# Rooms of attention's first operands in SBUF reordered, and mLSTM steps begun 0.3 heads later

## The chip, the cores and the metric

One core of a Trainium2 chip runs the whole program, one decoder block over 2048 tokens. The metric is the time of one execution in microseconds (us). A core has five engines that work side by side: TensorE (PE, matmuls and transposes into PSUM), VectorE (DVE), ScalarE (ACT), GpSimd (POOL) and SyncE (SP), which here only issues DMA transfers. Each engine works through its own list of instructions strictly in order, and waits at the head of the list until what that instruction needs has happened.

## The reference, cut to what matters

The block computes a normalised hybrid mixer, a memory cross-attention and a mixture of experts:

```
z = rms_norm(x) @ w_in                      # input projection, split into
aq, ak, av, mu, mv, mo, mi, mf = split(z)   # attention and mLSTM parts
y_att = dilated_attention(rope(aq), rope(ak), av)     # 8 heads of 64
hc = mlstm_chunkwise(q(conv(mu)), k(conv(mu)), mv, mi, mf)  # 4 heads of 128
y_m = sigmoid(mo) * (norm(hc) + skip * conv(mu))
x += concat(y_att, y_m) @ w_out
x += cross_attention(rms_norm(x), rms_norm(mem))
x += hierarchical_moe(rms_norm(x));  out = rms_norm(x)
```

An attention head mixes three causal windows: 128 keys at stride 1 (set A in the kernel: 16 blocks of 128 queries against at most 256 keys), and the strides 4 and 16 together (set B: 16 tiles in four residue classes). Each block is scores, mask, exponent, a transpose of the probabilities, and their product with v. The mLSTM group runs 16 steps (4 groups of chunks times 4 heads) that carry a state from group to group.

## The kernel before

Every large product is done in two halves of a number, high and low, so that three matmuls stand for one.

**Stages.** `in_proj` (line 84) computes z in two halves of the sequence and writes all its parts to DRAM scratch tensors. `heads` (line 832) then runs three things at once: `attention` (line 370), head after head; `mlstm` (line 689); and `out_m` (line 791), the mLSTM rows' share of the output projection, in two halves. `cross` and `experts` follow.

**Order.** A planner builds each engine's list: it simulates the engines and takes among the instructions whose inputs it believes ready the one of the lowest priority number. Attention is traced first, and `marks[h]` keeps the priority at which head h begins. `go(t, gen)` sets the priority to that of time t in heads (t = 2.5 is the middle of head 2) and runs one step of `mlstm` or `out_m` there. mLSTM steps stand at t = 5.5 i / 16, i = 0 to 15, steps of `out_m` from t = 2 to 7.3 and its second half up to 7.9. All loads and stores of these stages are issued by SP, in one list.

**Rooms.** A pool of tiles (`pool`, line 46) takes a stretch of each SBUF partition. Pools are stacked in the order in which they are opened, tags inside a pool in the order of their first use. The pools of `heads` lie on the bytes that the pools of `in_proj` left. With `reuse_waits="tile"` a tile waits only for the users of the earlier tiles on its own bytes. Worked out from the shapes, in KiB from the start of a partition (1 KiB of kept tiles lies first), `in_proj` left:

- 1 to 10: constants `p1c`, the identity matrix `a_ident` among them, which the gate rows' transposes (line 685) still read
- 10 to 22.6: weight stage `wr` (3 buffers); to 34.6: `xr` (3), one of which is `room1` of the small gate rows of `gates` (line 619)
- to 42.6: `sq` (2); to 43.6: `dg`; to 59.6: `qh`, `ql` (2 each), which the convolution uses last; to 61.7: `on`; to 65.7: `u`; to 69.7: `v`
- to 81.7: output tiles `o` (3), written by the output gates (`gate`, line 316) at the very end and stored to `z_mo` (line 325)
- to 131: weights `W`; to 205: the x splits `xh`, `xl`, read until the last gate matmul

Before the change `heads` lays on them: score and row tiles `p2s` (1 to 15), `kl0`, `kl1`, identity and masks (15 to 34.5), `PTA`, three pairs of transposed probabilities of set A (to 46.5), `qs`, `kk` of the even heads (to 62.5), `vA`, `vB` (to 78.5), `PTB` (to 98.5), `qs`, `kk` of the odd heads (to 114.5), and, last, the tiles of `out_m` and `mlstm`, on the x splits.

**Names.** `load_qk` (line 394) loads a head's `qs`, `kk` and `kl`, ten transfers of 256 KB. `kl` holds a zero half that POOL writes once (lines 391, 392). Line 438/439 are the score matmuls, 446 mask and maximum (DVE), 447 the exponent (ACT), 493 and 552 the transposes, 452/453 the copies into `PTA`/`PTB` (ACT the high half, DVE the low one), 511 and 564 the products with `vA`, `vB`. In an mLSTM step line 739 and 746 load, 755 is q times k, 761 a transpose, 770 to 774 the products.

Of the kernel before, what the change touches and what calls it, by code (L numbers as in the profile page):

```python
# [8 lines left out]
F32 = mybir.dt.float32  # L9
F32R = mybir.dt.float32r  # L10
# [5 lines left out]
P = 128  # L16
D = 1024
S = 2048
# [27 lines left out]
def pool(tc, ctx, name, bufs, space=None, side=None):  # L46
    kw = {} if space is None else {"space": space}
    return ctx.enter_context(tc.tile_pool(name=name, bufs=bufs, side=side, reuse_waits="tile", **kw))
# [321 lines left out]
def attention(tc, ctx, I, Z, K, marks):  # L370

    nc = tc.nc
    sp = pool(tc, ctx, "p2s", 2)
    cp = pool(tc, ctx, "p2c", 1)
    qp = [pool(tc, ctx, "p2q", 1)]
    vp = [pool(tc, ctx, "p2v" + x, 1) for x in "ab"]
    dp = pool(tc, ctx, "p2d", 1)
    qp.append(pool(tc, ctx, "p2r", 1))
    op = pool(tc, ctx, "p2o", 1)
# [2 lines left out]
    ps_o = pool(tc, ctx, "p2po", NO, PSUM)  # L382

    def const(name, shape):
        t = cp.tile(shape, F32, name="b_" + name)
        nc.sync.dma_start(t, I[name])
        return t


    kls = [cp.tile([P, S], F32R, name=f"kl{x}") for x in range(2)]  # L390
    nc.gpsimd.memset(kls[0].bitcast(F32)[64:128], 0.0)
    nc.gpsimd.memset(kls[1].bitcast(F32)[0:64], 0.0)

    def load_qk(h):

        kl = kls[h % 2]
        qs, kk = (qp[h % 2].tile([P, S], F32R, name=f"{n}{h}", tag=n) for n in ("qs", "kk"))
        rows = slice(h * 64, h * 64 + 64)
        own, other = (slice(x * 64, x * 64 + 64) for x in (h % 2, 1 - h % 2))
        for c in range(2):  # L400
            cs = slice(c * 1024, c * 1024 + 1024)
            nc.sync.dma_start(qs.bitcast(F32)[own, cs], Z["qkh"][0, rows, cs])
            nc.sync.dma_start(qs.bitcast(F32)[other, cs], Z["qkl"][0, rows, cs])
            for to in (own, other):
                nc.sync.dma_start(kk.bitcast(F32)[to, cs], Z["qkh"][1, rows, cs])
            nc.sync.dma_start(kl.bitcast(F32)[own, cs], Z["qkl"][1, rows, cs])
        return qs, kk, kl
# [10 lines left out]

    first = load_qk(0)
    ident, mA, mB = const("ident", [P, P]), const("maskA", [P, 256]), const("maskB", [P, 512])  # L420
    K["ident"] = ident

# [49 lines left out]
    for pair in range(4):  # L472
# [3 lines left out]
        for e in range(2):  # L476
            h = 2 * pair + e
            marks.append(tc.cur_priority)
            qs, kk, kl = load_qk(h) if h else first
# [61 lines left out]
            for r in range(4):  # L541
# [15 lines left out]
                for kt in range(4):  # L557
                    for x in range(2):
                        if kt == 0:
                            t = pt[x][:, 1]  # L560
# [271 lines left out]
def heads(tc, I, Z, K):  # L832

    marks = []
    with ExitStack() as ctx:
        attention(tc, ctx, I, Z, K, marks)
        pb = pool(tc, ctx, "p3pb", NB, PSUM)

        def go(t, gen):

            j = int(t)
            tc.cur_priority = marks[j] + int((marks[j + 1] - marks[j]) * (t - j))
            next(gen, None)

        with ExitStack() as c2:
            o = out_m(tc, ctx, I, Z, pb, 0, 1)
            next(o)
            m = mlstm(tc, c2, I, Z, K, pb)
            next(m)
            at = [(MEND * i / 16, 0, i) for i in range(16)] + [(OSTART + (OMID - OSTART) * i / 16, 1, i) for i in range(16)]  # L850
            done = 0
            for t, which, i in sorted(at):

                while which and done < min(16, i // 4 * 4 + 5):
                    go(t, m)
                    done += 1
                if which or i == done:
                    go(t, (m, o)[which])
                    done += not which
        o = out_m(tc, ctx, I, Z, pb, 1, 2)  # L860
        for i in range(17):
            go(OMID + (OEND - OMID) * i / 16, o)
        tc.cur_priority = max(marks[9], tc.cur_priority)
        return marks[8]
# [3 lines left out]
WARM = 9  # L868
NS, NT, NO, NB = 2, 2, 2, 2
NPA, NPB = 3, 2  # L870
MEND, OSTART, OMID, OEND = 5.5, 2, 7.3, 7.9


def mm3(nc, out, wh, wl, xh, xl, first, last):
# [973 lines left out]
def block_kernel(tc, I, out):  # L1848
    with ExitStack() as ctx:
        Z = scratch(tc, ctx)  # L1850
        K = keep(tc, ctx)
        in_proj(tc, I, Z, K)
        soon = heads(tc, I, Z, K)
        router = Router(tc, ctx, I, Z)
        cross(tc, I, Z, router, soon)
        experts(tc, I, Z, router, out)
# [14 lines left out]
```

## Time and profile before

| | us |
|---|---|
| median of 3 runs | 2208.98 (2201.88 to 2212.25) |
| the profiled execution | 2215.31 |
| its span | 2213.5 |

The page's busy line gives each engine's busy time, its share of the span and its instructions. A table by stage gives, for each stretch, its length, then busy time and count of PE, of the weight loads (PEld), DVE, ACT and POOL, then the mean granted clock of PE (1.00 is full speed), the mean busy share of the 16 DMA engines, and GB/s moved. A list of waits says which instruction stood for what. A timeline gives start, duration, engine, line, operands and count, and in brackets the idle time before it and what ended it.

### The profile page before, as it was taken

What the parts mean: (1) busy time and instruction counts of PE and PEld (TensorE: products, weight loads), DVE (VectorE), ACT (ScalarE), POOL (GpSimd) and SP (SyncE); (2) the same over time, 40 slices, a digit from 0 to 9 for tenths busy, and PEclk for the clock granted to TensorE, in tenths of its full rate; (3) what the DMA queues carried; (4) which work ended last, traced back from release to release, by engine and by line L of the source; (5) the groups of instructions that cost most, each with busy time, mean ns of one, the idle gap of its engine ahead of it and who ended that gap; (6) DMA issues with size and microseconds to landing.
All of it is one profiled execution on the core that took longest, in us unless ns stands there. A gap on an engine that the chain in (4) does not pass through costs nothing. (4 is left out here: it accounts for less than half of the span.)

```text
span 2213.5 us, 36146 instructions
## 1 busy us (share of the span) xinstructions
PE 2041.5 (92%) x13247; PEld 1875.2 (85%) x13247; DVE 1373.3 (62%) x3315; ACT 1043.4 (47%) x2216; POOL 635.0 (29%) x415
## 2 busy tenths in 40 slices
PE   8999999999888888889969999858999999999996
PEld 6898988988677888879968999857999998889985
DVE  8125741255278889865688788865666565445576
ACT  5223432233266766665534545425555554444462
POOL 3541235421344454543240020142111111121003
PEclk9999999999899999999979999968999999999998
DMA  7544645342697897786552222257878786666596
GB/s 205 178 154 142 215 144 155 113 131 111 174 236 195 242 234 216 208 228 182 180 175 72 100 96 87 87 156 239 247 222 251 202 240 193 168 188 179 152 337 236
DMA packets 276244, 402.45 MB, mean 182 GB/s; under 512 B 28176, under 2 KB 204624, under 8 KB 276016
## 3 DMA queue, kind: packets, MB, share of 16 engines
q1 hardware_dynamic: 262528, 355.11, 52.3%
q0 software_dynamic: 13536, 45.00, 8.3%
q8 instruction: 106, 1.74, 0.3%
q14 instruction: 74, 0.61, 0.1%
HBM read 286.33 MB, written 114.00 MB: 181 GB/s over the span
## 5 line engine op out<-in xcount | busy, mean ns | idle before, releaser
L39 POOL TENSOR_TENSOR wl<-wr,wh 128x1024 fp32r<-128x1024 f32 (+1 forms) x46 | 118.9, 2606 | 256.0 <-ACT wh L38 244.0
L1654 POOL DMA_INDIRECT z_acc<-y,ix x34 | 55.9, 1645 | 407.2 <-DVE y L1646 175.5
L876 PE MATMUL pa<-xl,ww_0h 128*128 128x256 f32 (+5 forms) x512 | 153.0, 307 | 2.2 <-DVE xl L42 2.2
L875 PE MATMUL pa<-xh,ww_1h 128*128 128x256 f32 (+5 forms) x512 | 152.0, 297 | 0.0
L877 PE MATMUL pa<-xh,ww_1l 128*128 128x256 f32 (+5 forms) x512 | 151.7, 296 | 0.0
L876 PE MATMUL pa<-xl,ww_1h 128*128 128x256 f32 (+5 forms) x512 | 151.6, 296 | 0.0
L877 PE MATMUL pa<-xh,ww_0l 128*128 128x256 f32 (+5 forms) x512 | 147.6, 299 | 0.0
L335 PE MATMUL pn<-wl,xh 128*128 128x256 f32 (+1 forms) x512 | 144.9, 283 | 0.0
L334 PE MATMUL pn<-wh,xh 128*128 128x256 f32 (+1 forms) x512 | 144.9, 283 | 0.0
L336 PE MATMUL pn<-wh,xl 128*128 128x256 f32 (+1 forms) x512 | 144.9, 283 | 0.0
L42 DVE SCALAR_TENSOR_TENSOR xl<-pt,f_gf,xh 128x256 fp32r<-128x256 f32 (+5 forms) x128 | 64.3, 515 | 116.5 <-ACT xh L41 116.1
L875 PE MATMUL pa<-xh,ww_0h 128*128 128x256 f32 (+5 forms) x512 | 135.4, 301 | 0.6 <-ACT xh L41 0.6
L41 ACT ACTIVATE xh<-pt,f_gf 128x256 fp32r<-128x256 f32 (+5 forms) x128 | 61.9, 499 | 135.6 <-PE pt L1576 135.2
L38 ACT CAST wh<-wr 128x1024 fp32r<-128x1024 f32 (+3 forms) x49 | 48.4, 1030 | 130.5 <-PE pn L336 58.0
L39 DVE TENSOR_TENSOR ww_1l<-ww_1r,ww_1h 128x512 fp32r<-128x512 f32 x124 | 77.6, 676 | 46.3 <-ACT ww_1h L38 46.2
L876 PEld LDWEIGHTS pa<-xl,ww_0h 128*128 128x128 f32 x512 | 97.8, 192 | 4.8 <-DVE xl L42 2.4
L877 PEld LDWEIGHTS pa<-xh,ww_0l 128*128 128x128 f32 x512 | 97.6, 192 | 0.9
L335 PEld LDWEIGHTS pn<-wl,xh 128*128 128x128 f32 x512 | 97.1, 190 | 0.9
L334 PEld LDWEIGHTS pn<-wh,xh 128*128 128x128 f32 x512 | 97.1, 190 | 0.9
L336 PEld LDWEIGHTS pn<-wh,xl 128*128 128x128 f32 x512 | 96.9, 189 | 0.5
L875 PEld LDWEIGHTS pa<-xh,ww_1h 128*128 128x128 f32 x512 | 97.4, 190 | 0.0
L877 PEld LDWEIGHTS pa<-xh,ww_1l 128*128 128x128 f32 x512 | 97.2, 190 | 0.0
(708 smaller groups left out, 7140.3 us busy)
## 6 DMA issues: line engine op xcount, KB each, us to landing
ww_1r<-w SPq DMA_DIRECT2D x31, 1024.0 KB
ww_0r<-w SPq DMA_DIRECT2D x30, 1024.0 KB
wr<-w_in SPq DMA_DIRECT2D x43, 512.0 KB
w_0r<-w SPq DMA_DIRECT2D x16, 1024.0 KB
w_1r<-w SPq DMA_DIRECT2D x16, 1024.0 KB
z_v<-v SPq DMA_DIRECT2D x32, 256.0 KB
z_mqk<-mq SPq DMA_DIRECT2D x16, 512.0 KB
kk<-z_qkh SPq DMA_DIRECT2D x32, 256.0 KB
```

The costliest lines, as they stand in the source:

```text
L38: a = nc.scalar.copy(hi, src)
L39: b = eng.tensor_sub(lo, src, hi.bitcast(F32))
L41: a = nc.scalar.activation(hi, src, AF.Copy, scale=scale)
L42: b = eng.scalar_tensor_tensor(lo, src, scale, hi.bitcast(F32), op0=OP.mult, op1=OP.subtract)
L334: nc.tensor.matmul(ps[:, :n], xhw, wh[:, k, :], start=(k == 0), stop=False)
L335: nc.tensor.matmul(ps[:, :n], xhw, wl[:, k, :], start=False, stop=False)
L336: nc.tensor.matmul(ps[:, :n], xlw, wh[:, k, :], start=False, stop=(k == KT - 1))
L875: nc.tensor.matmul(out, wh, xh, start=first, stop=False, skip_group_check=True)
L876: nc.tensor.matmul(out, wh, xl, start=False, stop=False, skip_group_check=True)
L877: nc.tensor.matmul(out, wl, xh, start=False, stop=last, skip_group_check=True)
L1654: d = nc.gpsimd.indirect_dma_start(out=Z["acc"], out_offset=bass.IndirectOffsetOnAxis(ap=self.ix[:r, n:n + 1], axis=0), in_=y[:r], in_offs ...
```

## The change

It opens three pools first, a new one (`ip`) for the `kl` tiles, the identity and the masks, then that of the even heads' `qs` and `kk`, then those of `vA` and `vB`; the score tiles and the pool of `PTA` come after them. All sizes stay, so everything from `PTB` on lies where it lay. The new places, in KiB: `kl0`, `kl1` 1 to 17, identity and masks to 20.5, `qs`, `kk` to 36.5, `vA` to 44.5, `vB` to 52.5, score tiles to 66.5, `PTA` to 78.5. And mLSTM steps stand at t = 0.3 + 5.2 i / 16. No instruction is added or removed.

```diff
 def attention(tc, ctx, I, Z, K, marks):
 
     nc = tc.nc
+
+    ip = pool(tc, ctx, "p2i", 1)
+    qp = [pool(tc, ctx, "p2q", 1)]
+    vp = [pool(tc, ctx, "p2v" + x, 1) for x in "ab"]
     sp = pool(tc, ctx, "p2s", 2)
     cp = pool(tc, ctx, "p2c", 1)
-    qp = [pool(tc, ctx, "p2q", 1)]
-    vp = [pool(tc, ctx, "p2v" + x, 1) for x in "ab"]
     dp = pool(tc, ctx, "p2d", 1)
...
     def const(name, shape):
-        t = cp.tile(shape, F32, name="b_" + name)
+        t = ip.tile(shape, F32, name="b_" + name)
...
-    kls = [cp.tile([P, S], F32R, name=f"kl{x}") for x in range(2)]
+    kls = [ip.tile([P, S], F32R, name=f"kl{x}") for x in range(2)]
...
-            at = [(MEND * i / 16, 0, i) for i in range(16)] + [(OSTART + (OMID - OSTART) * i / 16, 1, i) for i in range(16)]
+            at = [(MSTART + (MEND - MSTART) * i / 16, 0, i) for i in range(16)] + [(OSTART + (OMID - OSTART) * i / 16, 1, i) for i in range(16)]
...
-MEND, OSTART, OMID, OEND = 5.5, 2, 7.3, 7.9
+MSTART, MEND, OSTART, OMID, OEND = 0.3, 5.5, 2, 7.3, 7.9
```

## Rows read from the trace of the kernel before

**Rows 1.** The page: span, and busy time of each engine

```profile
span 2213.5 us, 36146 instructions
PE 2041.5 (92%) x13247; PEld 1875.2 (85%) x13247; DVE 1373.3 (62%) x3315; ACT 1043.4 (47%) x2216; POOL 635.0 (29%) x415
```

**Rows 2.** Table by stage, columns as above: head 0 to its B, head 1, end

```profile
588.16:632.73 44.57, 27.82 (x168) 24.56 (x167) 20.57 (x74) 16.38 (x49) 12.60 (x10) 0.77 1.07 268
...
657.74:717.74 60.00, 51.33 (x349) 46.26 (x348) 49.13 (x163) 42.30 (x120) 26.20 (x21) 0.97 0.81 199
...
1022.41:1085.00 62.59, 62.09 (x484) 61.21 (x483) 39.34 (x106) 37.50 (x96) 11.99 (x5) 1.00 0.54 163
```

**Rows 3.** PE's waits, 585 to 640 us: total, times, longest

```profile
PE pst L755 <- DMA kT<-z_mqk: 6.0, 1, 6.0
PE oA L511 <- DMA vA<-z_v: 5.1, 1, 5.1
PE sA L438 <- DVE stA L446: 2.5, 3, 1.7
```

**Rows 4.** PE's timeline in head 0

```profile
588.78 0.33 PE L438 MATMUL sA<-kk,qs 128*128 128x128 f32 x1 [0.61 <-DVE g L224]
...
600.63 2.04 PE L755 MATMUL pst<-qT,kT 128*128 128x128 f32 x8 [5.97 <-DMA kT<-z_mqk]
...
605.87 0.39 PE L438 MATMUL sA<-kk,qs 128*128 128x256 f32 x1 [0.21 <-DVE stA L446]
...
607.92 0.39 PE L438 MATMUL sA<-kk,qs 128*128 128x256 f32 x1 [0.63 <-DVE stA L446]
...
612.57 1.16 PE L755 MATMUL pst<-qT,kT 128*128 128x128 f32 x8
...
620.16 0.39 PE L774 MATMUL po<-v,kT 128*128 128x129 f32 x2
...
625.64 0.55 PE L511 MATMUL oA<-ptah,vA 128*128 128x256 f32 x1 [5.09 <-DMA vA<-z_v]
...
632.73 0.42 PE L438 MATMUL sB<-kk,qs 128*128 128x128 f32 x1
```

**Rows 5.** DVE's timeline, its first reduction

```profile
590.99 0.29 DVE L446 CUSTOM_DVE_ANT_0 pA<-sA,b_maskA 128x128 f32<-128x128 f32 x1 [1.64 <-DMA b_maskA<-maskA]
```

**Rows 6.** SP's timeline of issues, 560 to 616 us

```profile
566.55 0.58 SPq L325 DMA_DIRECT2D z_mo<-g  x1
573.33 0.34 SPq L682 DMA_DIRECT2D decb<-z_dec  x1
573.77 0.47 SPq L402 DMA_DIRECT2D qs<-z_qkh  x1
...
592.32 0.38 SPq L739 DMA_DIRECT2D kT<-z_mqk  x1
...
601.24 0.32 SPq L325 DMA_DIRECT2D z_mo<-g  x1
...
611.27 4.54 SPq L483 DMA_DIRECT2D vA<-z_v  x4
```

**Rows 7.** Table by stage, stretches of 5 us

```profile
570.00:575.00 5.00, 5.00 (x24) 4.14 (x23) 0.00 (x0) 0.00 (x0) 1.51 (x1) 1.00 0.00 0
...
585.00:590.00 5.00, 4.37 (x22) 3.28 (x21) 1.32 (x4) 0.60 (x1) 0.00 (x0) 1.00 1.06 218
590.00:595.00 5.00, 2.96 (x13) 2.59 (x13) 2.77 (x13) 3.52 (x13) 2.77 (x1) 0.70 1.06 327
595.00:600.00 5.00, 0.00 (x0) 0.00 (x0) 0.21 (x1) 0.48 (x2) 0.00 (x0) 0.50 1.02 256
600.00:605.00 5.00, 4.37 (x20) 4.40 (x21) 1.03 (x3) 0.00 (x0) 2.50 (x2) 0.50 1.06 371
...
625.00:630.00 5.00, 4.36 (x23) 4.39 (x23) 1.63 (x5) 2.03 (x4) 0.00 (x0) 0.55 0.96 258
```

**Rows 8.** POOL's timeline: last weight split; kl zeroed; last gate tile

```profile
514.54 5.75 POOL L39 TENSOR_TENSOR wl<-wr,wh 128x1024 fp32r<-128x1024 f32 x2 [17.80 <-ACT wh L38]
...
573.49 1.81 POOL L391 MEMSET kl<- 64x2048 f32 x1 [14.87 <-DMA z_mo<-g]
...
590.54 2.77 POOL L324 TENSOR_SCALAR g<-g 128x1024 f32<-128x1024 f32 x1 [7.91 <-ACT g L323]
```

**Rows 9.** PE's waits, 1080 to 1145 us

```profile
PE psk L1013 <- POOL ssmem L1006: 8.4, 1, 8.4
```

## The prediction

> **What bounds the kernel now.** I read the page's busy lines first: TensorE (PE) is busy 92% of a span of 2213.5 us, VectorE (DVE) 62% [rows 1]. So an edit is worth something only where PE stands or runs slowly. The change touches one seam, the end of the input projection and the start of attention, so the table by stage comes next. From the last gate matmul (588.16 us) to the first score of head 0's second window set B (632.73), PE is busy 27.82 of 44.57 us at a mean granted clock of 0.77, and DVE only 20.57 us; in the next whole head (657.74 to 717.74) PE is busy 51.33 of 60 us at 0.97 and DVE 49.13 [rows 2]. The reader is to see that the first 45 us are poor and that afterwards DVE and PE are both near full. At head 1's DVE rate (49.13/60 = 0.82) the 20.57 us of DVE work would need 25 us. The first stretch is thus about 44.6 - 25 = 20 us behind the pace that this kernel keeps later. That is the ceiling of what can be won.
>
> Who ends the waits there? PE's list names two transfers: kT of the first mLSTM step, 6.0 us, and vA of head 0, 5.1 us; then 2.5 us for row statistics on DVE [rows 3]. The timeline shows the order: scores of head 0 from 588.78, a hole up to 600.63 that ends with an mLSTM matmul, and a hole up to 625.64 that ends with the first product with vA [rows 4]. DVE's own first reduction waits 1.64 us for the mask [rows 5]. SP's queue says why vA is late: it is issued at 611.27, after mLSTM's loads (kT at 592.32) and after the last store of the gates (601.24) [rows 6]. By the code the rooms of vA and vB are the projection's output tiles, which the gates store last; so the planner puts vA behind that store. Head 0's q and k are issued from 573.77, right behind the read of the decay row, 573.33 [rows 6], though DMA is idle from 570 to 575 (share 0.00) and full from 595 on (1.02 and more) [rows 7].
>
> **The change, part by part.**
>
> vA and vB move from the output tiles to rooms of the squares, keys and q splits, which the convolution leaves long before the gates end. vA can then be issued with head 0's other operands, some 35 us before 611.27, and is first needed four to five blocks into head 0. Removed: the wait of 5.1 us [rows 3]. Bounds: 0 (it stays queued where it is) to -5.1; I take -5.1, since nothing else of its room is late.
>
> The mLSTM steps begin at 0.3 of head 0 and not at 0. Before, PE's order held a step-0 matmul whose kT was issued at 592.32 and arrived for 600.63 [rows 6, 4]; it couldn't be issued sooner, because its room is that of the x splits that PE reads until 588.16. In the change the scores go first. A pair of A blocks takes about 2.1 us (605.87 to 607.92) [rows 4], so the eight pairs of A last 17 us and 0.3 of a head is some five pairs, or 10 to 12 us: the step is wanted at about 600, when kT was there before too. The 6.0 us go, with 1 us left for nb, iwb and v behind it: -5. Bounds: 0 to -6.0. Every load of the step moves with it; SP has only to issue them later, and the queue they leave holds head 1's q and k, needed much later.
>
> The constants move to the weight stage's rooms, last read at 514.54 + 5.75 = 520.3 us [rows 8]. The mask's 1.64 us wait [rows 5] goes: -1.6 (0 to -1.6). The zeroing of the kl tiles waits on POOL until 573.49 [rows 8]; in their new room they wait for the projection's identity matrix, whose last use is in the gate rows' transposes some us before that. It saves nothing by itself, as the scores cannot start before PE has finished the gates at 588.16.
>
> The clock. Around the two holes PE is granted 0.70 in 590 to 595, 0.50 in 595 to 605 and 0.55 in 625 to 630, where 0.50 is the lower level, 1.2 of 2.4 GHz; in the 5 us before it was 1.00, with PE busy 4.37 of them [rows 7]. What ran there would have taken its busy time by its clock: 2.96 x 0.30 + 4.37 x 0.50 + 4.36 x 0.45 = 5.1 us less. That is the ceiling; without the holes most of it comes back: -4.5 (0 to -5.1).
>
> Added: with no mLSTM matmul to fill in, head 0 runs A alone for some five pairs. Beside the pair of 605.87 PE waits 0.21 and 0.63 us for statistics [rows 4]; the products with vA will fill some of that, so I take 0.6 us a pair, 5 x 0.6 = 3 us in which PE stands where steps 0 and 1 ran before: +3 (0 to +16, if both displaced steps, 8 us each from 612.57 to 620.55 [rows 4], find no gap later).
>
> Added: the transposed probabilities (PTA) now lie in the output tiles. The copy that fills the last of the three pairs must wait until the last gate store has been read out. POOL finishes that tile at 590.54 + 2.77 = 593.3 [rows 8]. What a 512 KB store takes until its waiters go on is seen once: issued at 566.55, SP's and POOL's next waits end at 573.3 to 573.5, 6.9 us [rows 6, 8]. So it is free at about 600; the tag's 51 tiles (3, then 24 in each half) go round three buffers, so the last sits in the third, whose first 0.8 KB lie under the third pair of PTA. That pair is wanted after the fourth pair of blocks, 589 + 4 x 2.1 = 597.5: a stall of some 2 us, +1.7 (0 to +7, if it lies under the first pair). On ACT and DVE the exponents and reductions of the next blocks queue behind that copy, and PE waits for them.
>
> The Trainium skill, "DMA: Bandwidth & Descriptors", Anatomy of one DMA, gives about 2.0 us plus bytes over 436 GB/s, which as an estimate is 3.2 us for this store; the row's 6.9 us is twice that and decides. By the page the stall would be nil and the sum 2 us lower.
>
> Sum: -5.1 - 5 - 1.6 - 4.5 + 3 + 1.7 = -11.5 us. The profiled run took 2215.31 us (1.8 us around its span); it becomes 2203.8. The median of the runs shown is 2208.98, 6.3 us under that, so the median becomes 2197.5. Later stages take the shift over: the end of the heads stage is PE at 62.09 of 62.59 us [rows 2], so that idle PE time saved earlier counts whole, and cross-attention's own hole (8.4 us for ssmem) [rows 9] hangs on what the heads release.
>
> **The rivals.** About 0.5%, 11 us, is what a measurement of this kernel can tell from no change.
>
> *More than the sum.* vA, vB, the constants and part of q move into the idle DMA stretch before 573 and the whole lag shrinks to a ramp of 3 us: -17, 2192. For it: share 0.00 there [rows 7]. Against: SP takes its list in order and stood behind the gate rows until 573.33.
>
> *DMA is the bound.* The share is 1.07 on average over the 44.57 us, at 268 GB/s [rows 2]: 11.9 MB. If the order of loads changes but the bytes wanted by the start of B don't, only clock and mask are won, less the 3 us of A alone: -4.5 - 1.6 + 3 = -3, 2206. Against it: the 2.6 MB of head 1's q, k and kl are among these bytes and not wanted until 657.74, and at 600 to 605 the same queue moved 371 GB/s [rows 7]. The Trainium skill, same page, Bandwidth, puts the limit at about 358 GB/s for a core; by it, as an estimate, 11.9 MB need 33 us and 11 us of the stretch are free, by the row's 268 none.
>
> *The gate store under the first pair of PTA.* The whole copy chain stands until 600, so 7 us are lost in place of 1.7: -6, 2203.
>
> *Nothing moves.* The planner leaves vA behind the gate stores, and what the later step frees is spent waiting for it: only the mask's 1.6 us go, less what A loses alone, -1, 2208. For it: q and k had free rooms before, too, and were still issued at 573.77 [rows 6].
>
> *Slower.* The displaced steps are the price. A step now comes every 0.325 of a head instead of 0.344, in heads where DVE has 49.13 of 60 us filled [rows 2]. If the two steps that ran in the holes find no gap there they cost 2 x 8 = 16 us, and the output projection behind them, which wants whole chunks of mLSTM rows, slips by as much; less 5 us for vA, +11 or more, 2220. It decides if head 1 or 2 grows by more than 8 us. Against it: step 15 is due at 5.18 heads, before at 5.16, and the last 63 us are output-projection work on a full PE, which takes up what comes late.
>
> **How the numbers follow.** The sum 0.47, with 2191 to 2204 as its own range; more than the sum 0.14; DMA bound 0.11; store under the first pair 0.08; nothing moves 0.07; slower 0.13. Faster by over 0.5%, below 2198, are the larger case and a good half of the sum's: 0.14 + 0.26 = 0.40; slower 0.13; the rest, 0.47, lies within. The range 2188 to 2213 leaves out the slower case and the far end of the larger one.
>
> **What would show it.** Right: vA and vB issued before 595; no PE wait for vA; the first mLSTM matmul after the fourth or fifth pair of A; B of head 0 starting near 620 instead of 632.73; a clock of 0.9 or more from 590 to 630; head 1 no longer than 62 us. Wrong: a copy into PTA waiting for the gate store beyond 600; the same holes under other names with DMA share over 1.0; or heads 1 to 5 each longer by 2 us or more.

## The result and the profile after: 0.7% slower, not 0.5% faster

The changed kernel takes 2221.21 us in the median (2218.89 to 2238.37) against 2208.98 us; the ratio over all their runs is 1.0068, with a 95% interval of [1.0048, 1.0088] (that of the medians alone is 1.0055). 2197.5 was forecast, in a range up to 2213, with 0.13 on slower.

The page of the changed kernel: its span, and busy us of each engine. The profiled execution took 2221.28 us, 5.97 more than that of before. The counts of the five engines are those of [rows 1].

```profile
span 2219.4 us, 36127 instructions
PE 2034.4 (92%) x13247; PEld 1874.0 (84%) x13247; DVE 1368.5 (62%) x3315; ACT 1044.3 (47%) x2216; POOL 632.4 (28%) x415
```

Its table by stage, columns as in [rows 2]: first A score to first B score of head 0, head 1, end of the heads.

```profile
588.10:631.29 43.19, 22.01 (x135) 20.04 (x136) 15.31 (x53) 15.78 (x46) 11.23 (x8) 0.68 1.08 275
...
659.53:716.21 56.68, 46.75 (x330) 43.45 (x328) 47.78 (x161) 37.17 (x109) 21.13 (x18) 0.94 0.81 205
...
1028.89:1085.00 56.11, 55.64 (x436) 54.98 (x437) 35.64 (x98) 34.73 (x88) 12.16 (x6) 1.00 0.60 183
```

[rows 2] starts its first stretch 0.6 us earlier, at the last gate matmul. From the first A score on it took 43.95 us before, so the stretch is 0.8 us shorter now; PE is busy 5.8 us less in it, at a clock of 0.68 instead of 0.77, with the DMA engines as full as before (1.08). B of head 0 begins at 631.29, where 620 was forecast. PE's waits say what stands there now (585 to 640 us; total, times, longest):

```profile
PE pst L757 <- DMA kT<-z_mqk: 16.6, 1, 16.6
PE po L772 <- issue: 2.3, 1, 2.3
PE sA L440 <- DVE stA L448: 1.5, 1, 1.5
```

The wait for vA (5.1 in [rows 3]) is gone. The wait for kT has not gone from 6.0 to 1 but grown to 16.6 us. PE's timeline shows the place: after four pairs of A scores. Before, the step stood behind the same four pairs, whose last matmul [rows 4] leaves out:

```profile
594.24 0.41 PE L439 MATMUL sA<-kl,qs 128*128 128x256 f32 x1
```

The start of step 0 has not moved in the list. The kernel after:

```profile
588.10 0.33 PE L440 MATMUL sA<-kk,qs 128*128 128x128 f32 x1 [0.61 <-DVE g L224]
...
592.62 0.28 PE L441 MATMUL sA<-kl,qs 128*128 128x256 f32 x1
609.47 2.05 PE L757 MATMUL pst<-qT,kT 128*128 128x128 f32 x8 [16.57 <-DMA kT<-z_mqk]
...
619.02 0.57 PE L513 MATMUL oA<-ptah,vA 128*128 128x256 f32 x1
...
622.57 1.06 PE L757 MATMUL pst<-qT,kT 128*128 128x128 f32 x8
...
631.29 0.42 PE L440 MATMUL sB<-kk,qs 128*128 128x128 f32 x1
```

What has moved stands behind it. A's first product with vA (619.02) now runs ahead of step 1 (622.57); in [rows 4] step 1 (612.57) ran ahead of that product (625.64).

SP's issues say why kT came later (start, duration):

```profile
572.90 0.47 SPq L404 DMA_DIRECT2D qs<-z_qkh  x1
...
584.51 4.10 SPq L485 DMA_DIRECT2D vA<-z_v  x4
589.33 1.78 SPq L325 DMA_DIRECT2D z_mo<-g  x1
591.15 4.14 SPq L487 DMA_DIRECT2D vB<-z_v  x4
...
600.95 0.43 SPq L741 DMA_DIRECT2D kT<-z_mqk  x1
```

vA goes out 26.8 us earlier than in [rows 6], and vB with it, both ahead of kT, which slips from 592.32 to 600.95. Two tiles of 128 x 2048 f32 are 2.1 MB; at the stretch's 275 GB/s that is, as an estimate, 7.6 us, near the slip of 8.6.

The whole heads stage splits into head 0 and the rest, to the first matmul behind the heads (same columns). Before:

```profile
588.78:657.74 68.96, 51.19 (x314) 46.21 (x314) 43.73 (x148) 38.71 (x115) 29.28 (x23) 0.85 0.97 257
657.74:1097.33 439.59, 387.87 (x2739) 364.20 (x2737) 337.55 (x1004) 284.72 (x772) 194.45 (x142) 0.96 0.77 208
```

After:

```profile
588.10:659.53 71.43, 47.54 (x286) 44.33 (x286) 39.05 (x135) 38.28 (x111) 25.05 (x20) 0.76 0.87 226
659.53:1107.57 448.04, 392.73 (x2767) 372.15 (x2765) 341.30 (x1019) 285.96 (x775) 198.62 (x146) 0.95 0.78 208
```

Head 0 is 2.5 us longer although it holds 28 matmuls less, all of them mLSTM's (three steps are transposed in it, not four); PE stands idle for 23.9 us in it (length less busy) instead of 17.8. The rest is 8.4 us longer: 28 matmuls more, idle 55.3 instead of 51.7 us, and a slightly lower clock. So two sums have to be explained, one in head 0 and a larger one after it. Together they are 10.9 us, and the two spans differ by only 5.9: the part behind the heads, where the change does nothing, took 1111.8 us in this profile, 1116.2 in that of before and 1111.0 in that of e12 below, so 4.3 us of scatter hide in the comparison of the spans.

### The profile page after: what moved, and what is told of

It reads as the page before. It is cut to its first block, busy times and chain, and to the rows that moved or that the text cites. A ratio compares the mean times of both kernels' runs of the same rounds, so it can differ in the third digit from the quotient of the medians.

```text
span 2219.4 us, 36127 instructions
## 1 busy us (share of the span) xinstructions
PE 2034.4 (92%) x13247; PEld 1874.0 (84%) x13247; DVE 1368.5 (62%) x3315; ACT 1044.3 (47%) x2216; POOL 632.4 (28%) x415
## 3 DMA queue, kind: packets, MB, share of 16 engines
q1 hardware_dynamic: 262528, 355.11, 52.5%
## 5 line engine op out<-in xcount | busy, mean ns | idle before, releaser
L878 PEld LDWEIGHTS pa<-xl,ww_1h 128*128 128x128 f32 x512 | 97.9, 191 | 0.0
```

What stands on the lines that cost most here:

```text
L878: nc.tensor.matmul(out, wh, xl, start=False, stop=False, skip_group_check=True)
```

## Experiments

Behind each run stand its median and its ratio to the kernel before, with a 95% interval.

**Rooms alone, start alone.** e1 is the changed kernel with the old start of the steps, e2 the kernel before with the new one.

```diff
-MSTART, MEND, OSTART, OMID, OEND = 0.3, 5.5, 2, 7.3, 7.9
+MSTART, MEND, OSTART, OMID, OEND = 0.0, 5.5, 2, 7.3, 7.9
```

> The new rooms with the mLSTM steps at their old places (5.5 i / 16). Theory A (order of loads): vA and vB go ahead of the first mLSTM step's kT in the one list of transfers, while PE's list still holds that step's first matmul behind the fourth pair of A blocks; the whole loss is made at the seam by the rooms. Then this run is as slow as the change: 1.004 to 1.009 of before, with one wait for kT of 15 to 18 us and none for vA. Theory B (pitch): the closer pitch of the steps costs in heads 2 to 7, and the rooms alone are no loss: 0.997 to 1.002. Theory C (PTA on the output tiles): as A in time, but a copy into PTA waits past 600 us for the gate store.

> The old rooms with the mLSTM steps begun 0.3 heads later. Theory A: nothing is won or lost at the seam, because the planner places step 0 by what it believes ready and not by its priority: holes of 6 us for kT and 5 us for vA as before, B of head 0 at 631 to 634, time 0.998 to 1.002 of before. Theory B: 1.004 to 1.009, with heads 2 to 7 longer by 10 us in sum.

e1: 2235.26 us, 1.0111 [1.0077, 1.0144], with kT's hole at 16.4 us and PE's and SP's lists at the seam as in the changed kernel. e2: 2215.65 us, 1.0016 [0.9996, 1.0036], kT's hole 6.9 and vA's 4.3 us, near those of before. The rooms alone make the loss, in e1 more of it than the 1.004 to 1.009 expected. The start does nothing at the seam, where PE's list is the same with either value: the planner takes what it believes ready. With the new rooms the later start seems to help a little further on (e1 is slower than the changed kernel, though the two intervals overlap).

**Holding step 0 back.** e3 queues PE's work of step 0 behind the last A score of head 0; e7 its work on DVE and ACT as well. The cut shows e3's edit at the first product; the transposes have the same.

```diff
-                nc.tensor.matmul(pst[:, i], kT[:, ws], qT[:, ws], start=True, stop=True)
+                with ExitStack() as order:
+                    if u == "0_0":
+                        order.enter_context(tc.issue_after(K["last"].ins))
+                    nc.tensor.matmul(pst[:, i], kT[:, ws], qT[:, ws], start=True, stop=True)
```

> The change, with the first matmuls and transposes of mLSTM step 0 held on PE behind the last pair of A's scores in head 0. Theory A: no wait for kT of more than 3 us, A done before 612, B of head 0 from 615 to 622 in place of 631.3, and 6 to 12 us faster than the change: 0.997 to 1.003 of before. Theory B: the seam is better but the later heads give it back, 1.003 or more. Theory C: a hole of 5 us or more stays before 605, for a copy into PTA.

> The changed kernel, with all of step 0's compute (PE, DVE and ACT) held in the lists behind the last block of A scores of head 0, where e3_hold held PE's alone and left ACT's four exponents ahead. Theory A-seam (the loss is the seam's hole): no list stands on kT any more, no hole over 6 us is left in A of head 0, the first B score starts at 616 to 622 instead of 631, and the time is 2207 to 2213 (0.999 to 1.002 of before). Theory D (the steps' lag is what is paid: the end of the heads follows the last step): the first transposes of a step come at 618 to 630, as late as in e3_hold, the last at 940 or later, the heads end 12 to 20 us later than before, and the time is 2222 to 2235 although the seam is smooth.

e3: 2233.13 us, 1.0093 [1.0061, 1.0124]; e7: 2235.19 us, 1.0109 [1.0082, 1.0135]. Neither smoothed the seam. The hole of e3 has another name, as PE's timeline and ACT's waits (585 to 640 us) show:

```profile
616.22 0.96 PE L515 MATMUL oA<-ptah,vA 128*128 128x256 f32 x2 [23.21 <-ACT ptah L456]
```

```profile
ACT nb L763 <- POOL nb L752: 20.3, 2, 16.8
```

ACT's list still had the four exponents of step 0, and three of step 1's, ahead of the copy that A's first product needs, so A stood for the steps' loads through ACT. In e7 a hole of 23.1 us is left at the same place. Step 0's exponents are held there (633.55), but step 1's, which the run did not hold, stand ahead of the copy and wait for step 1's nb (idle time in brackets):

```profile
615.87 0.98 ACT L766 ACTIVATE nb<-nb,colt 128x128 f32<-128x128 f32 x3 [21.01 <-POOL nb L754]
```

Holding one step on one engine, or one step of two, only moved the wait. In both runs the first transposes of a step come later than in the changed kernel (624.24 and 625.90 us against 611.31), and neither is faster than it. What a smooth seam with late steps costs, which e7 was to show, stays open.

**One room put back.** e4 leaves vB in its old place behind PTA, e9 both vA and vB (shown here); the other moves stay.

```diff
     qp = [pool(tc, ctx, "p2q", 1)]
-    vp = [pool(tc, ctx, "p2v" + x, 1) for x in "ab"]
     sp = pool(tc, ctx, "p2s", 2)
     cp = pool(tc, ctx, "p2c", 1)
+    vp = [pool(tc, ctx, "p2v" + x, 1) for x in "ab"]
```

> The change, with vB alone laid where the output tiles were (behind PTA) and vA in its new room. vB's load then falls behind the loads of mLSTM step 0. Theory A: kT is issued about 4 us earlier and its queue is 1 MB shorter, so the hole for kT shrinks from 16.6 to 8 to 11 us; 3 to 8 us faster than the change, 0.999 to 1.004 of before. Theories B and C: no more than 2 us faster than the change.

> The changed kernel with one of its four moves undone: vA's and vB's pools stand behind the statistics and PTA again (as before the change); constants, kl, qs and kk keep their new rooms, and the steps still begin 0.3 heads later. Theory V (the whole loss comes from the early rooms of vA and vB, through which their eight transfers go ahead of kT and PE's list takes A's products before mLSTM's steps): kT is issued at 591 to 594 us as before, the hole for it is 5 to 7 us and one of 4 to 5 us for vA comes back, PE stands idle for 16.5 to 18.5 us in head 0 instead of 23.9, and the ratio to before is 0.998 to 1.003. Rival (the other moved rooms or the later start share in the loss): head 0's idle time is 20 us or more, or it is 17 and later heads lose again; ratio 1.004 to 1.010.

e4: 2224.79 us, 1.0059 [1.0042, 1.0077], with kT issued at 597.27 and a hole of 11.3 us. The hole came nearly as expected (8 to 11 us), the gain in time did not. e9: 2215.39 us, 1.0025 [1.0010, 1.0039], the lists at the seam as before, and PE's two waits are back:

```profile
PE pst L757 <- DMA kT<-z_mqk: 7.7, 1, 7.7
PE oA L513 <- DMA vA<-z_v: 6.1, 1, 6.1
```

One, two and no early v tiles give 11.3, 16.6 and 7.7 us for kT. The rooms of vA and vB carry most of the loss; the other moves and the later start together are left with 0.1 to 0.4%. PE's list goes with vA's room: in e1 and e4, as in the changed kernel, three steps are transposed before head 1 begins, in e9 four, as before.

**An earlier start of the loads.** In e5 (new rooms) and e6 (old rooms) POOL's queue issues the gate rows' small transfers and the stores of half 1, so that SP should be free 25 us earlier; e14 is e6 with kl's zeros written by DVE.

```diff
-    nc.sync.dma_start(Z["ml"], ml)                # and the other small transfers of gates
+    nc.gpsimd.dma_start(Z["ml"], ml)
-                    nc.sync.dma_start(Z["mo"][h * P:(h + 1) * P, sh], o)
+                    (nc.gpsimd if half else nc.sync).dma_start(Z["mo"][h * P:(h + 1) * P, sh], o)
```

> The changed kernel, with the small transfers of the gate rows and the gate stores of half 1 on POOL's queue instead of SP's, so that SP's queue reaches the loads of head 0 about 25 us earlier, in a stretch (545 to 573 us) in which the DMA engines stood idle. Theory A (the new rooms cost because vA and vB go ahead of kT in one crowded queue, and everything of mLSTM then lags): with the queue free, kT is there before it is wanted, the hole of 16.6 us at 609 is under 2 us, head 0 reaches its first B score by 622 instead of 631, and the time falls below the kernel before: about 2195 us, a ratio of 0.990 to 0.998. Rival B (the rooms cost through head 1 and the later heads, whatever the seam does; the counts of matmuls show 11 of the 15 us lost between 632 and 740): the seam gains its 9 us but head 1 loses again, 2210 to 2218 us. Rival C (POOL's queue is too slow for the gate rows, and decb comes later than 573): POOL's transfers stand before its own evacuations in the input projection, and the time is 2225 or more.

> The control of e5_new_rooms_early: the kernel before, with the same transfers moved from SP's to POOL's queue, rooms and start of the steps as before. Theory A (the rooms matter only through the order of loads in a crowded queue): the kernel before gains from the earlier loads as well, the two holes at the seam of 6.0 and 5.1 us shrink, about 2198 us (0.992 to 1.000 of before), and e5_new_rooms_early and this one lie within 0.5% of each other. Rival B (the rooms cost in head 1 and later, by themselves): this one is quicker than e5_new_rooms_early by 10 us or more. If the old rooms hold the loads (qs, kk and vA lie where the projection's tiles end last), loads here can't start earlier than 570, and this control gains less than 3 us while e5 gains 10 or more: then the new rooms are worth what the change was for, once the queue is free.

> e6 (old rooms, gate rows' transfers and the stores of half 1 on POOL's queue) with the zeros of kl written by DVE instead of POOL, where they stood behind decb's issue until 578 us. All loads of head 0 can then be issued before 572 us. Theory M: kT is issued by 584 us and vA as soon as its room is free, the hole for kT of 4.2 us in e6 goes, head 0's idle time is 14 us or less (e6: 16.9, before: 17.8), and the ratio to before is 0.994 to 0.999. Rival: head 0 gains, but the planner orders the rest anew and the total is that of e6, 0.998 to 1.003.

e5: 2230.07 us, 1.0082 [1.0059, 1.0105]; e6: 2210.07 us, 0.9997 [0.9980, 1.0013]; e14: 2216.29 us, 1.0040 [1.0024, 1.0055]. e5 didn't start its loads early. SP's first load of qs stood until 576.86, as its waits show:

```profile
SPq L404 <- DMA z_ml<-room: 11.8, 1, 11.8
SPq L404 <- DMA z_dec<-room: 11.5, 1, 11.5
SPq L404 <- DMA room<-z_mm: 9.3, 1, 9.3
```

The new room of qs and kk lies on the tile of the small gate rows, which is alive until the decay row has been stored. In e6 qs, in its old room, went out at 543, but the first load into kl stood until 575.85, by SP's waits for the same gate rows (z_dec<-room, 11.8 us): kl's old room, too, lies on that tile. So e14's edit could not do what it was for. The zeros that DVE writes there wait as well, and kl's load left at 577.66:

```profile
577.97 1.76 DVE L391 MEMSET kl<- 64x2048 f32 x1 [5.15 <-DMA z_dec<-room]
```

kT left at 587.93 us in e6 and at 589.68 in e14, against 592.32 before, and its hole is 4.2 us in both. e6 ended its heads about 10 us earlier in the profile, and its median is that of the kernel before. None of the three is a better version, and none shows what loads that are really early would be worth.

**Output projection later.** e8 begins out_m at 2.5 heads instead of 2.

```diff
-MSTART, MEND, OSTART, OMID, OEND = 0.3, 5.5, 2, 7.3, 7.9
+MSTART, MEND, OSTART, OMID, OEND = 0.3, 5.5, 2.5, 7.3, 7.9
```

> The changed kernel with out_m (half 0) beginning 2.5 heads after the first instead of 2, its end as it was. Theory D (steps lag 10 to 18 us, so out_m's first loads wait for a step's store that hasn't landed, and ACT and PE stand behind it in order): ACT's wait of 6.18 us for ymh at 718.7 and PE's hole of 5.80 us at 722.7 go, and the time falls by 4 to 8 us to 2213 to 2217 (1.002 to 1.004 of before). Rival (that wait is one of many; out_m's work is only moved to where there is less room): 2219 to 2226, as the changed kernel.

2239.37 us, 1.0125 [1.0095, 1.0155]: a miss. The wait that it was to remove is still there, in ACT's timeline, longer than before and at the same place; the later due time did not move this first read, and the heads ended later (1120.83 us, against 1107.57 in the changed kernel).

```profile
720.38 1.04 ACT L38 CAST ymh<-yml 128x1024 fp32r<-128x1024 f32 x1 [7.14 <-DMA yml<-z_ym]
```

**A queue of its own for kT.** e10 (new rooms) and e11 (old rooms) issue step 0's qT, kT, nb and iwb from ACT.

```diff
-                nc.sync.dma_start(t, src)
+                (nc.scalar if name in ("qT", "kT", "nb", "iwb") and u == "0_0" else nc.sync).dma_start(t, src)
```

> The changed kernel, with four of the loads of mLSTM's step 0 (qT, kT, nb, iwb) issued by ACT's queue, not behind vA, vB and the gate stores in SP's. PE's list at the seam is nearly that of the changed kernel (A's first products before the end of step 0). Theory K (kT's place behind vA and vB in SP's queue is the cost, and later stages only pass it on): kT is issued by 590 us instead of 601, its hole is under 4 us instead of 16.6, PE's idle time in head 0 falls from 23.9 to 15 to 19 us, and the ratio to before is 0.997 to 1.002. Rival L (it is the new order of the list, with mLSTM's steps 9 to 20 us later all through the heads): head 0 gains, but the steps lag and heads 1 and 2 lose the gain again; 1.004 to 1.008. Rival T (the 16 DMA engines are full from 580 to 632, share 1.07 to 1.11, so an earlier issue of kT lands hardly earlier or delays qs or vA by as much): kT's hole is 6 us or more, or equal holes open at qs or vA; 1.004 or more.

> The control of e10_kT_own_queue_new: the kernel before (rooms and start as they were), with the same four loads on ACT's queue. Theory K: the hole for kT of 6.0 us falls below 3, that for vA of 5 us stays, the ratio to before is 0.996 to 1.000, and e10 and e11 differ by under 0.4%. Rival L: e11 is quicker than e10 by 0.5% or more although neither waits for kT. Rival T: kT is issued earlier and waited for as long as before; 0.999 to 1.003.

e10: 2226.67 us, 1.0082 [1.0055, 1.0110]; e11: 2225.58 us, 1.0075 [1.0057, 1.0093]. Theory T comes nearest, by kT's issue and by the time. ACT's timeline in e10:

```profile
598.64 0.36 ACTq L741 DMA_DIRECT2D qT<-z_mqk  x1
601.50 0.33 ACTq L741 DMA_DIRECT2D kT<-z_mqk  x1
602.17 0.40 ACT L449 ACTIVATE pA<-pA,stA 128x128 f32<-128x128 f32 x1 [13.34 <-DMA vB<-z_v]
```

kT left no earlier than from SP (601.50 against 600.95), and meanwhile ACT stood 13.34 us at its own issues, by the profile until a transfer of vB had ended, with A's exponents behind them; in e11 kT left at 592.98 (592.32 from SP) and ACT stood 8.3 us, until one of qs. PE's wait for kT did shrink, to 3.9 and 1.1 us, as Theory K had it, but PE then waited 11.1 and 7.1 us for those exponents. Both kernels are 0.8% slower than before, the old rooms too, and these stands are the likeliest reason. That e10 and e11 lie together says nothing on the rooms, as ACT's stand, the longer one in e10, covers their price. The Trainium skill, "DMA: Bandwidth & Descriptors", section "Issuing engines are not separate DMA queues", says that transfers started by different engines run on the same 16 DMA engines and that a second issuer saves only issue time; the runs agree, and show that the issuer's own work can pay for it.

**Bytes and order taken apart.** So far 2.1 MB ahead of kT and a new order of PE's list had come together. e12 is the kernel before, its list unchanged, with 2.1 MB of idle transfers at the place where the changed kernel issues vA and vB. e13 is the changed kernel, its list at the seam unchanged, without those bytes: head 0's vA and vB are zeros, so head 0's attention output is left out.

```diff
+    with tc.issue_after(K["last"].ins):           # e12, behind maskB's load
+        for r in range(8):
+            nc.sync.dma_start(Z["dum"][r], Z["v"][:, 0:P].rearrange("(m r) c -> r m c", r=4)[r % 4])
...
+            if h == 0:                            # e13
+                nc.gpsimd.memset(VA.bitcast(F32), 0.0)
+                nc.gpsimd.memset(VB.bitcast(F32), 0.0)
```

> The kernel before, with eight transfers of 256 KB added in SP's queue right behind maskB's, from z_v to a scratch tensor that nothing reads: as many bytes as vA and vB have, at the place where the changed kernel issues these. PE's list is that of the kernel before. Theory M (megabytes: what costs is 2 MB through full DMA engines ahead of kT): kT is issued at about 600 us instead of 592, the hole for it is 12 to 17 us instead of 6.0, PE stands idle for 23 to 28 us in head 0 instead of 17.8, and the ratio to before is 1.003 to 1.007, near the changed kernel's. Theory O (order: what costs is that the new rooms let PE's list take A's products before the steps, and all steps lag): the hole at kT grows by less, or is made good within head 0 or 1, and the ratio is under 1.002.

> The changed kernel without the loads of vA and vB of head 0: both tiles are filled with zeros by POOL, so head 0's attention output is left out. Everything else, PE's list at the seam included, is as in the changed kernel. Theory M: kT is issued at about 592 us, its hole falls from 16.6 to 5 to 8 us, PE's idle time in head 0 from 23.9 to 13 to 18 us, and the ratio to before is 0.995 to 1.001. Theory O: the hole shrinks, but the steps come as late against the heads as in the changed kernel, heads 1 and 2 lose what head 0 gained, and the ratio is 1.003 to 1.007.

e12: 2214.80 us, 1.0027 [1.0011, 1.0044]. e13: 2217.19 us, 1.0029 [1.0013, 1.0045]. Each is less than half of the loss, neither theory is right alone, and their sum of 0.56% lies within the interval of the whole. Counted from the first A score, kT is issued after 3.5 us before, 12.9 in the changed kernel, 9.9 in e12 and 3.1 in e13. PE's wait for it, e12 first, then e13:

```profile
PE pst L758 <- DMA kT<-z_mqk: 13.8, 1, 13.8
```

```profile
PE pst L761 <- DMA kT<-z_mqk: 8.0, 1, 8.0
```

In e12 the wait for vA is still there, 4.6 us. The table by stage, cut like that above, says where each acts. e12:

```profile
586.90:660.66 73.76, 49.27 (x313) 44.30 (x314) 43.55 (x148) 38.75 (x115) 29.32 (x23) 0.86 0.99 268
660.66:1100.50 439.84, 385.34 (x2739) 362.43 (x2737) 334.57 (x1004) 284.95 (x773) 194.29 (x142) 0.97 0.75 208
```

e13:

```profile
586.61:652.65 66.04, 49.16 (x285) 45.53 (x286) 38.58 (x135) 38.53 (x111) 25.03 (x20) 0.79 0.80 210
652.65:1102.86 450.21, 392.89 (x2766) 371.81 (x2765) 344.02 (x1019) 286.15 (x776) 198.82 (x146) 0.94 0.77 207
```

The bytes act in head 0 alone: 73.76 us against 68.96, +4.8, with PE idle 24.5 instead of 17.8 us; the rest is 439.84 us against 439.59. The list gains in head 0 (66.04, with a step less in it) and loses later: 450.21 against 439.59, +10.6. Together -2.9 + 10.6 = +7.7 for the list with the other moves, +4.8 + 0.2 = +5.0 for the bytes; the changed kernel's two rows are 10.9 us longer than those of before. Two biases remain: e13 moves 2.1 MB less than the kernel before, so its +7.7 may understate the list's price; e12 moves 2.1 MB more, where the change only reorders, so its +5.0 may overstate that of the bytes. And each row is one profile, so that the split is rough.

By the times alone e13 could owe its loss to the other moves and the later start, which it shares with e9: there the list is the old one and the loss 0.25%, against 0.29%. The stretch behind head 0 tells them apart. First e9's, then that of e4, where vA's early room makes the list the new one:

```profile
658.08:1097.74 439.66, 391.71 (x2738) 368.61 (x2736) 330.28 (x1006) 284.79 (x773) 194.52 (x142) 0.95 0.76 209
```

```profile
659.01:1104.30 445.29, 395.23 (x2763) 373.58 (x2760) 341.80 (x1017) 284.25 (x774) 198.19 (x146) 0.95 0.77 209
```

With the old list it takes 439.5 to 439.8 us in four kernels (before, e2, e9, e12), with the new one 445.3 to 454.4 in four others (the changed kernel, e1, e4, e13). So the loss behind head 0 goes with the list and not with the bytes or the other moves. A part of it is work that moved there from head 0; the whole heads show what is left: 507.7 to 510.2 us with the old list (before, e2, e9), 513.6 with the old list and the bytes (e12), 516.3 with the new list without them (e13), 519.5 with both. What the list is worth in the median time is not measured by itself.

What the list loses is a step's position. Before, four steps are transposed in head 0 (602.47, 614.68, 632.37 and 652.58 us), in the changed kernel three (611.31, 626.05 and 647.99, the fourth at 662.62), and the last of the 16 comes later in e13, too, whose seam is better. PE's timeline at step 15, before and e12 first:

```profile
925.27 0.66 PE L761 MATMUL pk<-b_ident,kT 128*128 128x128 f32 x4
```

```profile
925.77 0.66 PE L764 MATMUL pk<-b_ident,kT 128*128 128x128 f32 x4
```

Then the changed kernel and e13:

```profile
935.89 0.60 PE L763 MATMUL pk<-b_ident,kT 128*128 128x128 f32 x4
```

```profile
932.02 0.60 PE L767 MATMUL pk<-b_ident,kT 128*128 128x128 f32 x4
```

The later lists wait for these steps. ACT's stands for a step's gate row nb and for out_m's first read of a step's rows, between 680 and 720 us, first in the kernel before, then in the changed one, then in e13 (in brackets: idle time, and what ended it):

```profile
687.17 1.28 ACT L756 ACTIVATE nb<-nb,colt 128x128 f32<-128x128 f32 x4 [2.03 <-POOL nb L748]
695.10 1.04 ACT L38 CAST ymh<-yml 128x1024 fp32r<-128x1024 f32 x1 [3.48 <-DMA yml<-z_ym]
```

```profile
688.94 1.28 ACT L758 ACTIVATE nb<-nb,colt 128x128 f32<-128x128 f32 x4 [6.15 <-POOL nb L750]
718.73 1.04 ACT L38 CAST ymh<-yml 128x1024 fp32r<-128x1024 f32 x1 [6.18 <-DMA yml<-z_ym]
```

```profile
682.24 1.28 ACT L762 ACTIVATE nb<-nb,colt 128x128 f32<-128x128 f32 x4 [5.90 <-POOL nb L754]
711.39 1.04 ACT L38 CAST ymh<-yml 128x1024 fp32r<-128x1024 f32 x1 [4.95 <-DMA yml<-z_ym]
```

With the new list they are 1.5 to 4.1 us longer, in e13 with its better seam too, and behind each PE has a hole of 4.9 to 6.0 us. That such stands make the later loss is read from the traces, not shown: no run took them away, and e8, which tried it for one, failed to. How much of the 10.6 us they hold, and how much the lower clock (392.89 us busy at 0.94 against 387.87 at 0.96), stays open.

## Why the prediction was wrong, step by step

The step that failed is the term of -5 for kT, with what the term of -5.1 for vA left out: the transfers that move forward push kT back. The second is that nothing was put down for the stages after head 0.

- *vA and vB go out early, -5.1:* right, vA at 584.51 and no wait left. That the same step would put 2.1 MB in front of kT was left out. e12 shows that it costs: 2.1 MB ahead of kT, in an unchanged list, make its hole 13.8 us and the kernel 0.27% slower.
- *kT, "the step is wanted at about 600, when kT was there before too", -5:* wrong twice. kT did not keep its time (issued at 600.95 instead of 592.32), and the start of the step did not move in PE's list (e1, e2). Instead of -5 the wait gave +10.6. Over both waits that is +5.5, where the sum had -10.1; of it +2.5 stayed in head 0, with 28 matmuls less there, and +4.8 in e12 by the bytes alone.
- *Mask, -1.6:* wrong. DVE still waits 1.41 us for it, because the constants are issued behind the ten loads of q and k, as they were.

```profile
590.08 0.29 DVE L448 CUSTOM_DVE_ANT_0 pA<-sA,b_maskA 128x128 f32<-128x128 f32 x1 [1.41 <-DMA b_maskA<-maskA]
```

- *The zeros of kl move earlier and save nothing by that:* right, POOL writes them at 565.85 instead of 573.49.
- *Clock, -4.5:* wrong, as it hung on the holes. The granted clock of the first stretch fell from 0.77 to 0.68. (The three products of its ceiling add to 5.0, not 5.1.)
- *A alone, +3, and the store under PTA, +1.7:* neither shows. A did not run alone, as step 0 stayed behind its fourth pair; PE waits 1.5 us for row statistics. No copy into PTA stands for the gate store. The 6.9 us that the term took for a 512 KB store are a misreading: SP's wait that ended at 573.33 was, by its list of waits before, for the small decay row, issued just ahead of that store, and in e14 kl's zeros wait for the same row. No run here shows what such a store takes.

```profile
SPq L682 <- DMA z_dec<-room: 6.1, 1, 6.1
```

- *Later stages take the shift over:* wrong, and the larger half of the loss. Head 1 is shorter (56.68 us, under the 62 given, with 19 matmuls less in it), but the heads after head 0 take 8.4 us more together, and 10.6 in e13, without the bytes of vA and vB.
- *The rivals and the signs.* "DMA is the bound" had the mechanism, a stretch whose bytes do not change at a share of 1.07, and priced it at -3, as if their order were free. "Slower", 2220, was nearest in time: displaced steps, out_m late behind them. The sign that was to decide for it is there: head 2 took 65.16 us instead of 54.53, though head 3 gave 8.1 us back. But the steps were displaced by A's products with V, not by the start of 0.3 heads, and by one step, not two, so its 2220 against 2221 is in part luck. Four signs for "right" came true beside a wrong sum. Two of them, early v tiles and no wait for vA, tested only that term; the place of the first mLSTM matmul was the same before, and head 1 was shorter with less work in it.

## What to carry to other kernels

A room that comes free earlier is also a place further forward in the queue of transfers. Where the DMA engines are full, list what each engine needs first and ask what the early transfer pushes back; here 2.1 MB wanted at 619 us went ahead of a tile wanted at 593. And a planner that places work by believed readiness may turn an earlier operand into another order of the whole list: look at that order, where due times and priorities may change nothing, before costing the wait that is removed.

## What the runs showed beside

Two executions of one kernel differ by more than the seam's effects (the kernel before lay between 2195 and 2219 us over nine runs), so that a profile with heads 10 us shorter, as in e6, need not mean a faster kernel. Ledgers here compare cuts of profiles; the verdicts rest on the medians and ratios.
